# Order of the lo parts and of the products with the values in an attention loop

## Chip, cores and metric

One core of a Trainium2 chip runs the whole kernel. The metric is the device time of one execution in microseconds (us). Five engines have queues of their own, which are worked off in order and wait for one another only through semaphores: TensorE (PE, matmuls and transposes by matmul; PEld are its weight loads), VectorE (DVE), ScalarE (ACT), GpSimd (POOL) and SyncE (SP, which here issues most transfers).

## What is computed

One layer of a decoder trunk in float32: x (1, 1024, 1024) is normalised and projected, goes through three branches (sparse attention, a convolution module, cross-attention into 256 memory tokens), is merged by sigmoid gates, and ends in a SwiGLU feed-forward part. The change lies in the sparse attention, which has 8 heads in 2 groups and three kinds of keys, added up by gates:

```python
s_c = einsum(qq, kc);  p_c = masked_softmax(s_c, cmp_end <= t);   o_c = p_c @ vc    # compressed blocks
idx = top_k(imp_s, 16)                                            # of 16 blocks: all of them
s_s = einsum(qq, ks[idx]);  p_s = masked_softmax(s_s, tok <= t);  o_s = p_s @ vs[idx]   # selected
s_w = einsum(qq, kw);  p_w = masked_softmax(s_w, 0 <= t - pos < 512);  o_w = p_w @ vw   # window
out = gate[0] * o_c + gate[1] * o_s + gate[2] * o_w
```

There are 16 blocks of 64 tokens and 16 are selected, so the selected branch is causal attention over all tokens.

## The kernel before

Every float32 operand of a matmul is taken in two parts: hi, a cast to a shorter format by ScalarE (line 131), and lo, the rest, `src - hi`, by VectorE or GpSimd (line 132). The helper `split` emits the two one behind the other, and all products are sums over hi and lo parts. `mm` (line 146) is the helper that records every matmul, so all of them show as L146; tiles tell them apart.

The attention runs over 16 units (i, g): i counts eight tiles of 128 queries, g the two groups of four heads. A unit takes four steps of the loop: window scores of heads 0 and 1, of heads 2 and 3, then selected scores of heads 0 and 1 (`hp` = 0) and 2 and 3 (`hp` = 1). `scores` makes the score products, the maxima (VectorE, L771; L760 for the 64 compressed keys, which come with the selected ones) and the exponentials (ScalarE, L776 and L762, recorded in `exps`). GpSimd multiplies by the reciprocal sum and the gate (L695).

What follows the scores is put on a list, `due`, under a later step. Four steps after the selected scores of a half come the products with the values, `values`. For a half of the selected branch it goes through the key tiles two by two (a "pair"; i + 1 tiles, so up to four pairs). For each pair:

- up to four transposes (PE, L890) turn the probabilities into a bank of PSUM of pool 1 (`at=1`, two banks, shared with the turned queries and the compressed probabilities);
- the cast (ACT, L131) and the lo part (DVE, L132) go to a tile of the pool `t4` (four buffers, also used for the hi parts of the window);
- per key tile, one product with the hi and one with the lo part are added to the output bank `OB[(i, g)]` (pool 2, two banks).

For the compressed branch all four heads are turned into one bank (L876, 64 partitions), split into the lower and upper 64 partitions of one tile, and one product with `vcmp` adds both parts. It is emitted ahead of the selected products of the first half and has the `start` flag that opens the output bank. Window probabilities take another way: VectorE turns them in squares (L808), SP stores them (L816) and loads them again (L828), GpSimd makes their lo parts, and `window_products` closes the bank. `heads_out` then adds the two halves of the bank (L861, L862) and stores the sum (L864).

Between all this lie fill products: the merge gates' projection, emitted with the lowest priority in banks `pf` (L146 pf, then L948). Each is tied to an entry of `anchors`, a list of products of the attention, so that the fills are spread over it. After the attention come the branches' output projections (L1014 to L1027).

The order of each engine's queue is not the order of emission. The context is opened with `schedule_with_timeline_sim=True`: a planner takes ready instructions by priority (order of emission, unless set otherwise) on a timeline of times that it estimates, gives out buffers as it goes, and so fixes the order of every queue. `follow(m, i, why)` adds to that planning an edge with no semaphore: m is planned behind i.

Of the kernel before, what the change touches and what calls it, by code (L numbers as in the profile page):

```python
# [8 lines left out]
F32 = mybir.dt.float32  # L9
F32R = mybir.dt.float32r  # L10
BF16 = mybir.dt.bfloat16
AF = mybir.ActivationFunctionType
OP = mybir.AluOpType
# [4 lines left out]
P = 128  # L18
# [15 lines left out]
WB, SPREAD = 6, 97  # L34
# [5 lines left out]
def hybrid_layer_kernel(  # L40
# [4 lines left out]
    nc = tc.nc  # L45
# [21 lines left out]
    def nm(s):  # L67
        count[0] += 1
        return f"{s}_{count[0]}"

    def slab(shape, dt=F32R):
        return slabs.tile([P] + shape, dt, tag="slab", name=nm("slab"))
# [13 lines left out]
    def t4(shape, dt=F32):  # L86
        return t4p.tile([P] + shape, dt, tag="t4", name=nm("t4"))

    def t2(shape, dt=F32, p=P):
        return t2p.tile([p] + shape, dt, tag="t2", name=nm("t2"))  # L90
# [8 lines left out]
    def bank(shape, dt=F32, p=P, at=None):  # L99
        if at is None:  # L100
            turn[1] += 1
            at = order[turn[1] % len(order)]
        return psp[at].tile([p] + shape, dt, tag=f"ps{at}", name=nm("ps"))
# [9 lines left out]
    def const(shape, dt, name, p=P):  # L113
        return cp.tile([p] + shape, dt, tag=name, name=name)
# [15 lines left out]
    def split(hi, lo, src, eng=None):  # L130
        m = nc.scalar.copy(hi, src)  # L131
        return m, (eng or nc.vector).tensor_tensor(lo, src, hi.bitcast(F32), op=OP.subtract)  # L132
# [12 lines left out]
    def mm(o, a, b, start, stop):  # L145
        m = nc.tensor.matmul(o, a, b, start=start, stop=stop)  # L146
        n = 1
        for d in o.shape[1:]:
            n *= d
        products.append((m.ins, n if a.dtype == F32R else 4 * n))  # L150
        return m
# [14 lines left out]
    ident = identr.bitcast(F32)  # L166
# [26 lines left out]
    vcmp = const([2, P], F32R, "vcmp")  # L193
# [9 lines left out]
    def follow(m, i, why):  # L203
        tc.add_manual_dep(m.ins, i.name, ORDER, reason=why)
# [164 lines left out]
    b = bank([2 * KT])  # L369
# [10 lines left out]
    for u in range(2):  # L380
        w_ = slab([2, 2, 512])
        m, _ = split(w_[:, 0], w_[:, 1], raw_w[u])
# [20 lines left out]
    b = bank([4, TAPS + 3])  # L403
# [5 lines left out]
    b = bank([2, 16])  # L409
# [45 lines left out]
    b = bank([NT, 24])  # L455
# [83 lines left out]
    for hp in range(2):  # L539
# [7 lines left out]
        b = bank([2, 256])  # L547
# [100 lines left out]
    VSW = [slab([NT, 2, P]) for _ in range(2)]  # L648
# [27 lines left out]
    with low(TAP):  # L676
        along = products[first_tap:]
        total, run, j = sum(n for _, n in along), 0, 0
# [18 lines left out]
    QS, OB, QN, PC, WT, WP, WF, anchors, behind, tails, exps = {}, {}, {}, {}, {}, {}, {}, [], [], [], []  # L697
# [24 lines left out]
    def turn_q(i, g):  # L722
        if g == 0 and i + 1 < NT:
            load_q(i + 1)
        qd = t2([4, 2, 64])
        nc.gpsimd.tensor_tensor(qd, QN[i][:, 4 * g:4 * g + 4, None, :].to_broadcast([P, 4, 2, 64]),
                                rqn[:, i, 4 * g:4 * g + 4, None, None].to_broadcast([P, 4, 2, 64]), op=OP.mult)
        b = bank([4, P], at=1)
        for h in range(4):
            nc.tensor.transpose(b[:, h, :], qd[:, h].rearrange("p a d -> p (a d)"), ident)  # L730
        QT = stage.tile([P, 2, 4, P], F32R, tag="st", name=nm("qt"))
        split(QT[:, 0], QT[:, 1], b)
        QS[(i, g)] = QT
# [86 lines left out]
    def window_load(i, g):  # L820
        full = min(i + 1, 4)
        WT[(i, g)] = slab([4, 4, 4, 32])
        for j0 in range(0, full, 2):
            square_load(WT[(i, g)][:, j0:min(j0 + 2, full)], i, g, j0)
# [33 lines left out]
    def heads_out(i, g):  # L858
        o = OB[(i, g)]
        bot = t2([4, P], p=64)  # L860
        nc.scalar.copy(bot, o[64:128])  # L861
        nc.vector.tensor_tensor(bot, o[0:64], bot, op=OP.add)  # L862
        put = lambda: follow(
            nc.sync.dma_start(od[2 * g:2 * g + 2, :, i * P:(i + 1) * P].rearrange("c (h d) t -> d (c h) t", d=64), bot),  # L864
            exps[-1], "stored behind the last exponential")
        due.setdefault(4 * (2 * i + g) + 10, []).insert(0, put)

    def values(u, tiles):
        i, g, br, hp = u
        if br == 0:  # L870
            OB[(i, g)] = bank([4, P], at=2)
        o = OB[(i, g)]
        if br == 0:
            b = bank([4, P], at=1)
            for h in range(4):
                nc.tensor.transpose(b[:64, h, :], tiles[h], ident)  # L876
            pt = t2([4, P], F32R)
            split(pt[:64], pt[64:], b[:64])
            m = mm(o.rearrange("p h q -> p (h q)"), vcmp[:, g, :], pt.rearrange("p h q -> p (h q)"), True, False)
            anchors.append((3, m.ins))  # L880
            return
        nb = i + 1
        oh = o[:, 2 * hp:2 * hp + 2, :].rearrange("p h q -> p (h q)")
        for j0 in range(0, nb, 2):
            js = range(j0, min(j0 + 2, nb))
            b = bank([2, 2, P], at=1)
            pt = t4([2, 2, 2 * P], F32R)
            for j in js:
                for h in range(2):
                    nc.tensor.transpose(b[:, j - j0, h, :], tiles[h][:, j * P:(j + 1) * P], ident)  # L890
            n = len(js)
            bv = b.rearrange("p j h q -> p j (h q)")
            split(pt[:, 0, :n], pt[:, 1, :n], bv[:, :n])
            for j in js:
                for hl in range(2):
                    m = mm(oh, VSW[0][:, j, g, :], pt[:, hl, j - j0, :], False, False)
        anchors.append((WB + nb, m.ins))

    load_q(0)
    turn_q(0, 0)  # L900
    due = {}
    for n in range(2 * NT):
        i, g = n // 2, n % 2
        for at, br, hp in ((0, 2, 0), (1, 2, 1), (2, 1, 0), (3, 1, 1)):
            step = 4 * n + at
            for f_ in due.pop(step, []):
                f_()
            if (br, hp) == (1, 0) and n + 1 < 2 * NT:
                turn_q((n + 1) // 2, (n + 1) % 2)
            tiles = scores(i, g, br, hp)  # L910
            if br == 2 and hp == 0:
                for late, what, j0 in ((7, window_parts, 0), (8, window_parts, 2), (8, window_products, 0),
                                       (9, window_parts, 4), (9, window_products, 2), (9, window_products, 4)):
                    due.setdefault(step + late, []).append(lambda f=what, i=i, g=g, j0=j0: f(i, g, j0))
                due[step + 9].append(lambda i=i, g=g: heads_out(i, g))
            if br == 2:
                continue
            if hp == 0:
                due.setdefault(step + 4, []).append(lambda i=i, g=g: window_load(i, g))
                due[step + 4].append(lambda u=(i, g, 0, 0): values(u, PC[u[:2]]))  # L920
            due.setdefault(step + 4, []).append(lambda u=(i, g, br, hp), tiles=tiles: values(u, tiles))
    tails.pop()(exps[-1])
    while due:
        for f_ in due.pop(min(due)):
# [10 lines left out]
    with low(FILL):  # L935
        for n_ in range(3 * KT):
# [3 lines left out]
            for h_ in range(2):  # L940
                ps = fbank([512])
                for k in range(KT):
                    first = mm3(ps, w[:, 0, k, :], w[:, 1, k, :], xn(0, k, h_), xn(1, k, h_), k == 0, k == KT - 1)
                    j = ((n_ - N_EARLY) * 2 + h_) * KT + k
# [55 lines left out]
    for n_, (br, wt) in enumerate(branches):  # L1000
        ins = nxt
        for dp in range(4):
# [5 lines left out]
            for d_ in (2 * dp, 2 * dp + 1):  # L1008
# [6 lines left out]
                for half in range(2):  # L1015
# [13 lines left out]
                    if n_ == 2:  # L1029
                        if d_ % 2 == 0:  # L1030
                            MG[half][dp] = slab([2, 2, 512])
                        m = MG[half][dp]
# [51 lines left out]
    js = [[None] * 2 for _ in range(4)]  # L1084
# [72 lines left out]
    for c in range(2):  # L1157
# [4 lines left out]
        for t in range(NT):  # L1162
# [17 lines left out]
            h = H[tp][:, tt, cs]  # L1180
# [231 lines left out]
```

## Time and profile before

| what | value |
|---|---|
| median of three runs | 1691.99 us (1691.52 to 1693.93) |
| profiled execution | 1692.24 us, its span 1690.5 us |
| mean granted TensorE clock | 0.997 |
| busy: PE, PEld | 1658.4 us, 1382.6 us |
| busy: DVE, ACT, POOL | 1061.2, 727.2, 583.8 us |
| attention loop | about 430 to 800 us of the span |

Rows of the profile name engine, line, operation and tiles (output <- inputs), with buffer numbers left out: `t` are tiles of t4 or t2, `ps` banks of PSUM, `slab` and `wsl` larger tiles. In a row of waits stand the sum in us, the number of times and the longest; in an order of time the start, the duration, and in brackets the idle time of the engine ahead of it and what ended it. In a group's row the busy time, the mean in ns of one, then the idle time ahead of them.

### The profile page before, as it was taken

The numbers are of one execution on the slowest core, as the hardware profiler recorded it, in microseconds if no ns is written. First come the engines' busy times: TensorE is split into PE (matmuls) and PEld (weight loads), VectorE is DVE, ScalarE is ACT, GpSimd is POOL, SyncE is SP. The second block draws the span as 40 slices with busy tenths as digits, with TensorE's granted clock in tenths as the row PEclk, the third lists the DMA queues.
The fourth block names the chain that finished last, engine by engine and source line by source line (L and its number), as shares of the span: only waits on it lengthen the run. The fifth ranks groups of instructions, "written<-read, shape, count | busy, mean of one in ns | idle before, by whom it ended". The sixth has DMA issues, their size and how long they took to land.

```text
span 1690.5 us, 22456 instructions
## 1 busy us (share of the span) xinstructions
PE 1658.4 (98%) x8064; PEld 1382.6 (82%) x8064; DVE 1061.2 (63%) x1811; ACT 727.2 (43%) x1340; POOL 583.8 (35%) x514
## 2 busy tenths in 40 slices
PE   7999999999999999999989999999999999999999
PEld 6887898888888888887868888788888888888887
DVE  6278897678456777766567535864544545466655
ACT  6311443343366767676446324532222222233332
POOL 0000000110167777674016401566556776400000
PEclk9999999999999999999999999999999999999999
DMA  8012443312155555456555223233233445793763
GB/s 283 34 40 88 156 138 112 112 57 87 43 144 151 153 172 158 138 152 200 188 193 172 90 87 107 87 121 98 94 106 123 163 144 187 276 399 119 234 223 125
DMA packets 217173, 243.23 MB, mean 144 GB/s; under 512 B 13332, under 2 KB 146756, under 8 KB 216038
## 3 DMA queue, kind: packets, MB, share of 16 engines
q1 hardware_dynamic: 210150, 229.22, 42.5%
q10 hardware_dynamic: 6912, 12.59, 2.0%
q8 instruction: 63, 1.03, 0.3%
q14 instruction: 48, 0.39, 0.1%
HBM read 171.50 MB, written 70.25 MB: 143 GB/s over the span
## 4 chain that ended last, share of the span: by engine, by line
PE 56%; DVE 2%; DMA 1%; ACT 1%; issue 1%; SPq 0%; POOL 0%; ACTq 0%
PE ps L146 35%; PE ps L1346 11%; PE pf L146 7%; PE pf L1346 1%; DVE slab L132 1%; PE ps L890 1%; SPq L816 0%; ACT slab L131 0%; DMA st<-md 0%; DMA t<-zd 0%; DMA st<-in_w_mem_out_dram 0%; DVE t L128 0%; PE ps L233 0%; ACT fz L948 0%; DVE slab L1181 0%
## 5 line engine op out<-in xcount | busy, mean ns | idle before, releaser
L146 PE MATMUL ps<-slab,wsl 128*128 128x512 f32 (+1 forms) x1580 | 351.6, 381 | 1.8 <-ACT wsl L131 0.7
L146 PEld LDWEIGHTS ps<-slab,wsl 128*128 128x128 f32 x1580 | 286.7, 188 | 60.7 <-ACT wsl L131 1.1
L146 PE MATMUL pf<-slab,fsl 128*128 128x512 f32 x1260 | 326.2, 399 | 4.5 <-DVE slab L971 2.6
L146 PEld LDWEIGHTS pf<-slab,fsl 128*128 128x128 f32 x1260 | 230.5, 189 | 51.4 <-ACT fz L948 4.4
L146 PE MATMUL ps<-slab,fsl 128*128 128x512 f32 x708 | 165.9, 390 | 0.0
L1242 DVE TENSOR_TENSOR t<-ps,t 128x512 f32<-128x512 f32 x130 | 89.0, 689 | 118.0 <-PE ps L146 116.9
L146 PEld LDWEIGHTS ps<-slab,fsl 128*128 128x128 f32 x708 | 132.6, 188 | 27.6
L422 DVE SCALAR_TENSOR_TENSOR slab<-slab,cw 128x1021 f32<-128x1021 f32 (+15 forms) x120 | 151.6, 1265 | 1.9
L146 PE MATMUL ps<-wsl,slab 128*128 128x512 f32 (+1 forms) x690 | 148.5, 362 | 0.0
L146 PE MATMUL ps<-slab,slab 128*128 128x512 f32 x532 | 139.2, 397 | 3.3 <-POOL slab L132 1.1
L146 PEld LDWEIGHTS ps<-wsl,slab 128*128 128x128 f32 x690 | 115.8, 189 | 18.6
L594 POOL TENSOR_SCALAR t<-t,sm 128x256 f32<-128x256 f32 x32 | 17.9, 578 | 298.9 <-DVE sm L590 281.8
L146 PEld LDWEIGHTS ps<-slab,slab 128*128 128x128 f32 x532 | 100.2, 190 | 25.5 <-DVE slab L225 1.8
L1346 PE MATMUL ps<-wsl 128*128 128x512 f32 x492 | 118.0, 389 | 0.0
L1346 PEld LDWEIGHTS ps<-wsl 128*128 128x128 f32 x492 | 92.4, 188 | 19.1
L146 PE MATMUL ps<-t,slab 128*128 128x256 f32 (+1 forms) x500 | 104.4, 313 | 0.8 <-DVE t L132 0.7
L132 DVE TENSOR_TENSOR wsl<-st,wsl 128x1024 fp32r<-128x1024 f32 x58 | 74.4, 1285 | 36.4 <-ACT wsl L131 36.2
L132 DVE TENSOR_TENSOR t<-ps,t 128x512 fp32r<-128x512 f32 (+2 forms) x120 | 77.3, 649 | 31.8 <-ACT t L131 31.0
L131 ACT CAST wsl<-st 128x1024 fp32r<-128x1024 f32 x58 | 60.9, 1050 | 84.0 <-PE ps L146 36.4
L146 PE MATMUL ps<-slab,qt 128*128 128x384 f32 (+6 forms) x400 | 93.6, 339 | 1.4 <-DVE sm L771 0.9
L146 PEld LDWEIGHTS ps<-t,slab 128*128 128x128 f32 x500 | 78.0, 189 | 9.5 <-DVE t L132 2.3
L131 ACT CAST t<-ps 128x512 fp32r<-128x512 f32 (+2 forms) x120 | 65.1, 554 | 44.1 <-PE ps L890 25.0
(255 smaller groups left out, 2763.7 us busy)
## 6 DMA issues: line engine op xcount, KB each, us to landing
t<-in_w_down_dram SPq DMA_DIRECT2D x70, 256.0 KB, 3.9
fst<-in_w_in_dram SPq DMA_DIRECT2D x24, 512.0 KB, 3.9
zd<-fz ACTq DMA_DIRECT2D x48, 256.0 KB, 2.5
slab<-wd SPq DMA_DIRECT2D x24, 512.0 KB, 4.8
t<-zd SPq DMA_DIRECT2D x24, 512.0 KB, 4.1
st<-in_w_gate_dram SPq DMA_DIRECT2D x22, 512.0 KB, 3.7
st<-in_w_up_dram SPq DMA_DIRECT2D x22, 512.0 KB, 4.2
ad<-t SPq DMA_DIRECT2D x44, 256.0 KB, 2.7
```

Of the source, the lines that this page charges most:

```text
L131: m = nc.scalar.copy(hi, src)
L132: return m, (eng or nc.vector).tensor_tensor(lo, src, hi.bitcast(F32), op=OP.subtract)
L146: m = nc.tensor.matmul(o, a, b, start=start, stop=stop)
L422: return nc.vector.scalar_tensor_tensor(acc[:, s:], u[:, :S - s], cw[:, ct, 30 - s:31 - s], acc[:, s:], op0=OP.mult, op1=OP.add)
L594: nc.gpsimd.tensor_scalar(pm[:, tt, h, :], pm[:, tt, h, :], rec[:, j:j + 1], 1.0, op0=OP.mult, op1=OP.mult)
L890: nc.tensor.transpose(b[:, j - j0, h, :], tiles[h][:, j * P:(j + 1) * P], ident)
L1242: nc.vector.tensor_tensor(o, a_, b_, op=OP.add)
L1346: nc.tensor.matmul(B[t], a_, b_, start=start and k == 0 and j == 0, stop=k == FH - 1 and j == 2, skip_group_check=True)
```

## The change

The cast of each selected pair stays where it was. Its lo part is no longer emitted with it, but put on a list `pend`, and emitted after the cast of the next pair, with a planning edge behind that cast; the pair's products with the values come behind the lo part. The first product of the first half of the selected branch has the `start` flag. The compressed probabilities are turned and cast behind the second half (`short_values`, one step later than before); their lo part and product are emitted at the beginning of the next step, planned behind the last exponential. Anchors are recorded with the products, now in their new order.

```diff
+    def flush(after):
+        todo = list(pend)
+        pend.clear()
+        for f_ in todo:
+            f_(after)
+
+    def low_part(o, b, hi, after):
+        follow(nc.vector.tensor_tensor(o, b, hi.bitcast(F32), op=OP.subtract), after, "low part behind the next cast")
+
+    def short_values(i, g):
+        tiles = PC[(i, g)]
+        b = bank([4, P], at=1)
+        for h in range(4):
+            nc.tensor.transpose(b[:64, h, :], tiles[h], ident)
+        pt = t2([4, P], F32R)
+        flush(nc.scalar.copy(pt[:64], b[:64]).ins)
+
+        def rest(after):
+            low_part(pt[64:], b[:64], pt[:64], after)
+            m = mm(OB[(i, g)].rearrange("p h q -> p (h q)"), vcmp[:, g, :], pt.rearrange("p h q -> p (h q)"), False,
+                   False)
+            anchors.append((3, m.ins))
+
+        pend.append(rest)
+
     def values(u, tiles):
         i, g, br, hp = u
-        if br == 0:
+        if hp == 0:
             OB[(i, g)] = bank([4, P], at=2)
         o = OB[(i, g)]
-        if br == 0:
-            b = bank([4, P], at=1)
-            for h in range(4):
-                nc.tensor.transpose(b[:64, h, :], tiles[h], ident)
-            pt = t2([4, P], F32R)
-            split(pt[:64], pt[64:], b[:64])
-            m = mm(o.rearrange("p h q -> p (h q)"), vcmp[:, g, :], pt.rearrange("p h q -> p (h q)"), True, False)
-            anchors.append((3, m.ins))
-            return
...
             bv = b.rearrange("p j h q -> p j (h q)")
-            split(pt[:, 0, :n], pt[:, 1, :n], bv[:, :n])
-            for j in js:
-                for hl in range(2):
-                    m = mm(oh, VSW[0][:, j, g, :], pt[:, hl, j - j0, :], False, False)
-        anchors.append((WB + nb, m.ins))
+            flush(nc.scalar.copy(pt[:, 0, :n], bv[:, :n]).ins)
+
+            def rest(after, js=js, j0=j0, n=n, pt=pt, bv=bv):
+                low_part(pt[:, 1, :n], bv[:, :n], pt[:, 0, :n], after)
+                for j in js:
+                    for hl in range(2):
+                        m = mm(oh, VSW[0][:, j, g, :], pt[:, hl, j - j0, :], hp == 0 and j == 0 and hl == 0, False)
+                if js[-1] == nb - 1:
+                    anchors.append((WB + nb, m.ins))
+
+            pend.append(rest)
...
-                due[step + 4].append(lambda u=(i, g, 0, 0): values(u, PC[u[:2]]))
             due.setdefault(step + 4, []).append(lambda u=(i, g, br, hp), tiles=tiles: values(u, tiles))
+            if hp == 1:
+                due[step + 4].append(lambda i=i, g=g: short_values(i, g))
+                due.setdefault(step + 5, []).insert(0, lambda: flush(exps[-1]))
```

More of the change, by code (lines that the diff above doesn't have):

```diff
@@ L892, in values @@
             bv = b.rearrange("p j h q -> p j (h q)")
-            split(pt[:, 0, :n], pt[:, 1, :n], bv[:, :n])
-            for j in js:
-                for hl in range(2):
-                    m = mm(oh, VSW[0][:, j, g, :], pt[:, hl, j - j0, :], False, False)
-        anchors.append((WB + nb, m.ins))
+            flush(nc.scalar.copy(pt[:, 0, :n], bv[:, :n]).ins)
[7 more added lines that the diff above has]
+            pend.append(rest)
     load_q(0)
     turn_q(0, 0)
-    due = {}
+    due, pend = {}, []
     for n in range(2 * NT):
```

## The prediction

> **What bounds the kernel now.** I read the page first (busy shares, then the chain), then the stretch that holds the attention loop in the table of windows, then the waits of that stretch one engine at a time, and last the order of time around two of the waits.
>
> ```profile
> PE 1658.4 (98%) x8064; PEld 1382.6 (82%) x8064; DVE 1061.2 (63%) x1811; ACT 727.2 (43%) x1340; POOL 583.8 (35%) x514
> PE 56%; DVE 2%; DMA 1%; ACT 1%; issue 1%; SPq 0%; POOL 0%; ACTq 0%
> ```
>
> ```profile
> core 0: us, PE busy (x) PEld busy (x) DVE busy (x) ACT busy (x) POOL busy (x), PEclk, DMA share, GB/s
> 430.00:800.00 370.00, 361.48 (x2009) 306.63 (x2007) 244.21 (x818) 247.40 (x605) 238.44 (x254) 1.00 0.50 147
> ```
>
> The reader is to see that TensorE (PE) sets the time and that the attention, about 430 to 800 us, is no exception: there the matmuls fill 361.48 of 370 us, VectorE 244 and ScalarE 247, at a granted clock of 1.00. So a matmul moved from one place to another is worth nothing; only stretches in which PE stands still are. Those are these (a wait of the weight load, PEld, and one of the matmul are two views of the same stop, so the two lists are not added):
>
> ```profile
> PEld ps L146 <- DVE t L132: 7.2, 14, 1.1
> PEld pf L146 <- ACT fz L948: 2.8, 8, 0.5
> PEld ps L146 <- DVE sm L771: 1.9, 5, 0.8
> PE ps L146 <- DVE t L132: 2.8, 8, 0.7
> ```
>
> The largest cause is "t L132" on VectorE, the lo part of a split. It holds PE 14 times. Which products wait is told by the groups of instructions from 430 to 830 us:
>
> ```profile
> L146 PEld LDWEIGHTS ps<-t,vcmp 128*128 128x128 f32 x16 | 3.0, 188 | 5.1 <-DVE t L132 4.9
> L146 PEld LDWEIGHTS ps<-t,slab 128*128 128x128 f32 x374 | 58.9, 189 | 7.4 <-DVE t L132 2.3
> ```
>
> So 4.9 us belong to the 16 products with the compressed values (those that open the output bank) and 2.3 us to the products that read selected (and window) probabilities. Two of the first kind and one of the second, in order of time:
>
> ```profile
> 661.04 0.19 PEld L146 LDWEIGHTS ps<-t,vcmp 128*128 128x128 f32 x1 [0.64 <-DVE t L132]
> ...
> 764.66 0.58 ACT L131 CAST t<-ps 64x512 fp32r<-64x512 f32 x1
> 764.67 0.68 DVE L862 TENSOR_TENSOR t<-ps,t 64x512 f32<-64x512 f32 x1 [0.72 <-ACT t L861]
> 765.28 0.73 DVE L771 CUSTOM_DVE_ANT_0 slab<-ps,strip,sm 128x512 f32<-128x512 f32 x1
> 765.70 0.58 ACT L131 CAST t<-ps 128x512 fp32r<-128x512 f32 x1
> 766.05 0.69 DVE L132 TENSOR_TENSOR t<-ps,t 64x512 fp32r<-64x512 f32 x1
> 766.07 0.30 PEld L146 LDWEIGHTS ps<-slab,qt 128*128 128x128 f32 x2 [0.43 <-DVE sm L771]
> 766.79 0.19 PEld L146 LDWEIGHTS ps<-t,vcmp 128*128 128x128 f32 x1 [0.42 <-DVE t L132]
> 779.67 0.57 ACT L131 CAST t<-ps 128x512 fp32r<-128x512 f32 x1
> 780.27 0.69 DVE L132 TENSOR_TENSOR t<-ps,t 128x512 fp32r<-128x512 f32 x1 [0.81 <-ACT t L131]
> 781.02 0.53 PEld L146 LDWEIGHTS ps<-t,slab 128*128 128x128 f32 x4 [0.42 <-DVE t L132]
> ```
>
> In the middle one the cast was ready at 765.24, but VectorE took the lo part at 766.05, behind two other instructions of its queue, and PE, which had the compressed product next, stood for 0.42 us. In the last VectorE itself stood 0.81 us for the cast, and PE 0.42 us for the lo part.
>
> **The change, part by part.** It adds and removes no engine work and no transfer: the same 64 + 16 casts and lo parts of selected scores, 16 + 16 of the compressed ones, the same transposes and products. Only positions change. The kernel's planner puts each queue in order from the order of emission and from times it estimates, so a new order of emission changes the order on PE, ACT, DVE and, behind them, on POOL and SP too.
>
> ```profile
> L132 DVE TENSOR_TENSOR t<-ps,t 128x512 fp32r<-128x512 f32 x64 | 43.6, 685 | 26.6 <-ACT t L131 26.4
> L132 DVE TENSOR_TENSOR t<-ps,t 64x512 fp32r<-64x512 f32 x16 | 10.9, 684 | 0.7 <-ACT t L131 0.2
> L132 DVE TENSOR_TENSOR t<-ps,t 128x256 fp32r<-128x256 f32 x16 | 6.7, 416 | 2.7 <-ACT t L131 2.6
> L131 ACT CAST t<-ps 128x512 fp32r<-128x512 f32 x64 | 36.8, 580 | 19.0 <-PE ps L890 18.3
> ```
>
> (1) Lo parts of selected pairs behind the next pair's cast. At present VectorE waits 26.4 + 2.6 us in these rows for the cast just ahead of the lo part. With a cast in between (580 ns) that wait should mostly go; VectorE is busy 244 of 370 us, so its own time is worth nothing, but what is queued behind it (maxima, L771, on which PE waited 1.9 us) comes sooner. I count none of this.
>
> (2) Selected products behind that lo part. PE meets, between a pair's transposes and its products, the next pair's four transposes and whatever the planner puts there. Removes the 2.3 us, and what could be late next is the transposes two pairs on, which need the bank (two of them, `at=1`) that the lo part releases.
>
> (3) Compressed values last, their lo part behind the last exponential of the step, their product a step later. A step is some 6.6 us here (from the compressed product at 661.04 to the fourth after it, at 766.79, are sixteen steps), against 0.68 us for the lo part: removes the 4.9 us. Late next: nothing before the window products, which end the bank.
>
> (4) The first selected product opens the bank: the `start` flag moves from one matmul to another, nothing on any engine. It also frees the selected products from the wait for all four compressed tiles.
>
> (5) Fill products are tied to anchors, which now sit on later products of the same pair; the count and weights stay, so I take 0, covered by the products that now stand ahead of them. If that cover failed, the row to look at is "pf L146", whose wait for ACT is 2.8 us now.
>
> The sum. How much streaming is lost in a stop lies between the matmul list and the weight-load list: 2.8 and 7.2 us. The row below (from the chain) gives 0.23 us for 512 columns.
>
> ```profile
> 760.57 2.75 PE pf L146 x12
> ```
>
> Ahead of the stop at 766.79 the weights of two score products came at 766.07; the two, of 448 columns, stream 0.40 us, to about 766.47, 0.1 us into the idle of 0.42 that began at 766.37. So about three quarters of the idle is real: 0.75 x 7.2 = 5.4 us, which I take.
>
> New waits: nothing in the trace shows a product behind a later cast. Bound from below by 0, from above by a full extra cast on every pair whose transposes need a bank still held: pairs per half are 1, 1, 2, 2, 3, 3, 4, 4 for the eight query tiles, so 24 pairs stand third or later in their half (1 + 1 + 2 + 2, times two halves, times two groups), 24 x 0.58 = 13.9 us. The nearest row is the present wait of transposes, which shows PE standing on L890 only 0.5 us in all, because fills lie between; I take 0.8 us. Net: -5.4 + 0.8 = -4.6 us. Against the profiled execution (1692.24 us; its span 1690.5 and 1.74 around it) that is 1687.6; that execution stands 0.25 us above the median of 1691.99, so 1687.4 against the median.
>
> ```profile
> L890 PE MATMUL ps<-identr,slab 128*128 128x128 f32 x288 | 45.0, 272 | 0.5 <-DVE qt L132 0.5
> ```
>
> [...] The change holds each selected bank for one more cast. [...] No run of the present order can show it, and the second rival prices it from rows.
>
> **Rivals.** First, no change that can be measured (0.2% is 3.4 us): the idle goes from the attention and comes back where something else ends last. For it speaks what follows the attention:
>
> ```profile
> 863.64 1.13 PE L146 MATMUL pf<-slab,ones 128*128 128x512 f32 x2 [1.74 <-ACT fz L948]
> 867.34 4.61 PE L146 MATMUL pf<-slab,fsl 128*128 128x512 f32 x12 [2.57 <-DVE slab L971]
> 872.53 0.74 PE L146 MATMUL ps<-slab,wsl 128*128 128x512 f32 x2 [0.59 <-DVE slab L1025]
> ```
>
> Here PE stands 1.74 + 2.57 + 0.59 = 4.9 us: the last fill's result goes to memory and back before the branch can use it. If the fills end as late as now, or the last pair's longer way to its output pushes this stretch by as much as was won, the sum is about 0: 1692. Against it: PE, not these transfers, carries 56% of the chain.
>
> Second, slower: selected pairs are held one cast longer, in the two `at=1` banks and in the four `t4` tiles, of which the window parts take up to two. Place: the transposes (L890) of pair three and on in a half, and their casts (L131). Price: 0.58 us for each of the 24, if no fill lies ready. It decides when more than (4.6 + 3.4) / 0.58 = 14 of them are uncovered; with 18 it is -4.6 + 10.4 = +5.8, 1697.8, with all 24, 1701. For it: ACT already waits for these transposes 18.3 us (row above). Against: fills are spread over the whole attention and the pairs in which two or fewer are wanted don't meet it.
>
> Third, a larger gain. The compressed transposes hold one of the two `at=1` banks for long, because half of them come early:
>
> ```profile
> 646.66 0.38 PE L876 MATMUL ps<-identr,t 128*64 128x128 f32 x2
> 653.60 0.38 PE L876 MATMUL ps<-identr,t 128*64 128x128 f32 x2
> ```
>
> Over 14 us pass from the first transposes to the product (661.04, above), and the selected pairs go through the other bank. Emitted last, they would leave both banks to the selected pairs. The rest of the list of the weight load's waits:
>
> ```profile
> PEld ps L876 <- POOL t L695: 1.4, 2, 1.2
> PEld ps L146 <- POOL slab L132: 1.4, 1, 1.4
> PEld ps L146 <- PE ps L146: 1.0, 2, 0.6
> PEld ps L890 <- DVE qt L132: 0.8, 1, 0.8
> PEld ps L730 <- issue: 0.8, 1, 0.8
> PEld ps L146 <- ACT qt L131: 0.6, 1, 0.6
> ```
>
> With the 7.2 + 2.8 + 1.9 above it comes to 17.9 us; if half of the 10.7 us that are not lo parts went as well, 1687.4 - 5.4 = 1682.0.
>
> **How the numbers follow.** Forecast 0.45 (its own range 1684.8, all 7.2 us gone, to 1689.2, only 2.8), of which I put 0.36 below the bound of 3.4 us and 0.09 within it; first rival 0.22; second 0.24; third 0.09. Faster 0.36 + 0.09 = 0.45, same 0.09 + 0.22 = 0.31, slower 0.24. The predicted time is the forecast's, 1687.4. The range reaches to the third rival below (1682.0 less some 1.5) and above to where the second has 18 to 20 of its 24: 1680.5 to 1698.5; cases of both signs hold it.
>
> **What would show it.** Right: "t L132" gone or under 2 us among PE's waits in the attention, no idle ahead of the products with the compressed values, VectorE's wait for "t L131" far below 29 us, and the end of the attention's products some 5 us earlier. Wrong: a wait of L890 on "DVE t L132", or of L146 "ps" on something new, of several us; ACT waiting more than 18 us on L890; or an attention that is shorter and a stretch after 860 us that has grown. The forecast also fails if the new order on POOL or SP moves the window stores and loads (L816, L828) so that window products wait for them.

## Result and profile after

The changed kernel takes 1708.98 us (1707.16 to 1711.87, four runs) against 1692.43 us: a ratio of 1.0095, interval 1.0082 to 1.0107, or 16.6 us slower. The forecast was 1687.4 us, faster, with a range to 1698.5. A trace is of one of the timed executions, not of the median: 1709.83 us here, and in the experiments below 1706.24 us with the queries in another pool and 1710.16 us with the last unit at once, each the slowest of its kind.

In the changed kernel the lines of the attention have moved: L890 is now L906 (transposes of the selected pairs), L876 is L881, the cast and the lo part of the selected pairs are L909 and L875 (those of the compressed probabilities L883 and L875), L948 is L972. Page, then the attention and what follows it:

```profile
PE 1667.8 (98%) x8064; PEld 1389.0 (81%) x8064; DVE 1062.0 (62%) x1811; ACT 731.9 (43%) x1342; POOL 580.2 (34%) x514
PE 73%; DVE 5%; DMA 2%; issue 2%; ACT 1%; POOL 1%; SPq 0%; DVEq 0%; POOLq 0%; ACTq 0%
```

```profile
430.00:800.00 370.00, 355.44 (x1943) 1.00 0.47 136
800.00:900.00 100.00, 92.25 (x405) 0.93 0.61 209
```

The columns of the second fence are the stretch, its length, PE's busy time with its count, granted clock, share of the transfers and GB/s. The work is the same (8064 matmuls), but between 430 and 800 us 66 fewer of them (1943 for 2009) got done, with 355.44 us busy for 361.48. Behind 800 us the kernel before had this:

```profile
800.00:900.00 100.00, 94.39 (x407) 0.98 0.58 193
```

In the attention PE's weight loads wait for other things than before:

```profile
PEld ps L146 <- DVE sm L771: 8.9, 13, 1.6
PEld ps L146 <- DVE t L875: 6.2, 16, 1.8
PEld ps L146 <- ACT qt L131: 5.1, 8, 0.9
PEld ps L906 <- DVE qt L132: 3.2, 10, 0.5
PEld ps L146 <- issue: 2.5, 4, 1.6
```

The wait for lo parts has only fallen from 7.2 to 6.2 us, and two waits have grown: for the maxima (L771) from 1.9 to 8.9 us, and for the turned queries (`qt`, cast and lo part) from 0.6 + 0.8 to 5.1 + 3.2 us. The same by group, from 430 to 830 us:

```profile
L146 PEld LDWEIGHTS ps<-t,slab 128*128 128x128 f32 x361 | 61.3, 189 | 15.0 <-DVE t L875 8.3 <-ACT t L909 0.5
L146 PEld LDWEIGHTS ps<-t,vcmp 128*128 128x128 f32 x15 | 2.8, 188 | 0.9 <-DVE t L875 0.5
```

The compressed products hardly wait any more (4.9 to 0.5 us), as forecast; the selected products, which were to lose 2.3 us of waiting, now have 8.3, of which one stop at 810 us, behind the stretch above, is 2.6.

How the queries come late is seen in order of time, at the end of a first half (query tile 6, whose last pair has one key tile, so two transposes and a cast of 256):

```profile
722.24 0.38 PE L906 MATMUL ps<-identr,slab 128*128 128x128 f32 x2
...
722.91 0.36 ACT L909 CAST t<-ps 128x256 fp32r<-128x256 f32 x1
723.14 0.69 DVE L875 TENSOR_TENSOR t<-ps,t 128x512 fp32r<-128x512 f32 x1
...
724.34 0.60 PE L730 MATMUL ps<-identr,t 128*128 128x128 f32 x4
724.98 0.59 ACT L131 CAST qt<-ps 128x512 fp32r<-128x512 f32 x1 [0.42 <-PE ps L730]
725.62 0.47 PEld L146 LDWEIGHTS ps<-slab,qt 128*128 128x128 f32 x3 [0.76 <-ACT qt L131]
...
726.37 0.41 DVE L875 TENSOR_TENSOR t<-ps,t 128x256 fp32r<-128x256 f32 x1
```

The half's last pair is transposed at 722.24, and its lo part comes at 726.37: its bank is held for 4.5 us, though the cast was done at 723.27. The queries' transposes (724.34) come behind the lo part of the pair before (723.14 to 723.83), which frees the other bank, and the next score products need those queries at once: PE's weight loads stand 0.76 us for them, its matmuls 0.56.

### The profile page after: what moved, and what is told of

Same layout as the page of the kernel before. It is cut to its first block, busy times and chain, and to the rows that moved or that the text cites. A ratio compares the mean times of both kernels' runs of the same rounds, so it can differ in the third digit from the quotient of the medians.

```text
span 1708.1 us, 22461 instructions
## 1 busy us (share of the span) xinstructions
PE 1667.8 (98%) x8064; PEld 1389.0 (81%) x8064; DVE 1062.0 (62%) x1811; ACT 731.9 (43%) x1342; POOL 580.2 (34%) x514
## 4 chain that ended last, share of the span: by engine, by line
PE 73%; DVE 5%; DMA 2%; issue 2%; ACT 1%; POOL 1%; SPq 0%; DVEq 0%; POOLq 0%; ACTq 0%
PE ps L146 42%; PE pf L146 16%; PE ps L1370 11%; PE ps L906 1%; PE pf L1370 1%; DVE slab L771 1%; DVE slab L132 1%; DMA wd<-wsl 1%; ACT slab L131 1%; POOL slab L1052 1%; DVE wsl L808 1%; PE ps L604 0%; DMA t<-zd 0%; DVE t L875 0%; DMA st<-md 0%
## 5 line engine op out<-in xcount | busy, mean ns | idle before, releaser
L146 PE MATMUL ps<-slab,wsl 128*128 128x512 f32 (+1 forms) x1580 | 355.8, 384 | 1.2 <-ACT wsl L131 0.7
L146 PE MATMUL pf<-slab,fsl 128*128 128x512 f32 x1260 | 315.1, 394 | 1.5 <-ACT fz L972 1.5
L146 PE MATMUL ps<-t,slab 128*128 128x256 f32 (+1 forms) x500 | 118.3, 322 | 9.2 <-DVE t L875 8.9
L146 PEld LDWEIGHTS ps<-t,slab 128*128 128x128 f32 x500 | 82.9, 190 | 22.3 <-DVE t L875 13.2
L132 DVE TENSOR_TENSOR wsl<-st,wsl 128x1024 fp32r<-128x1024 f32 x58 | 75.7, 1306 | 37.9 <-ACT wsl L131 37.5
L132 POOL TENSOR_TENSOR slab<-slab,t 128x1024 fp32r<-128x1024 f32 (+1 forms) x28 | 62.6, 2235 | 65.7 <-ACT t L131 49.4
L146 PEld LDWEIGHTS ps<-slab,qt 128*128 128x128 f32 x400 | 63.7, 189 | 22.4 <-DVE sm L771 8.7
```

## Experiments

The theory I began with, 'bank held': a bank of the transposes that waits for a later cast before its lo part is one bank less for the next pairs and for the queries. Rivals: the later products themselves, the later place of the compressed probabilities, or lo parts at a bad place in VectorE's queue. Times are medians, ratios against runs of the kernel before on the same chip.

**Nothing deferred, compressed probabilities last.**

```diff
-            flush(nc.scalar.copy(pt[:, 0, :n], bv[:, :n]).ins)
+            cast = nc.scalar.copy(pt[:, 0, :n], bv[:, :n]).ins
...
-            pend.append(rest)
+            rest(cast)
```

(the same two lines in `short_values`)

> Nothing is deferred here: each lo part and its products follow their own cast, as before the change; what stays of the change is that the compressed probabilities come last, behind the second half, and that the first selected product opens the output bank. Theory 'bank held' (the two banks of the transposes are each held until the next pair's cast, so that pairs no longer overlap): this does not hold a bank longer, so within 5 us of before, 1687 to 1695 us, and PE waits less than 3 us for DVE sm L771. Theory 'compressed last' (the later place of the compressed probabilities makes the unit longer): 1703 us or more.

1689.01 us, ratio 0.9976 (0.9967 to 0.9985): faster. In the attention the weight loads' waits for L771 are 1.4 us, and the compressed products wait for no lo part. So the later place of the compressed probabilities and the new opening product are not the loss; alone they bring 3.4 us.

**The deferral alone.** `short_values` has `split` and its product at once, opens the bank, and stands ahead of the first half.

> The deferral alone: the compressed probabilities come first and open the output bank, as before the change; lo parts and products of the selected pairs come behind the next pair's cast, as in the change. Theory 'bank held': it has all of the cause, 1703 to 1713 us, with PE waiting over 5 us for DVE sm L771. Theory 'compressed last': 1688 to 1696 us.

1715.49 us, ratio 1.0134 (1.0118 to 1.0150). Slower than the change itself, so all of the loss is here, and a little above the range given:

```profile
PEld ps L146 <- ACT qt L131: 13.3, 12, 1.6
PEld ps L146 <- DVE t L875: 10.9, 22, 1.5
PEld ps L146 <- DVE sm L771: 7.1, 12, 1.2
```

The wait for turned queries is the largest of all.

**Lo parts with their casts, products deferred** (the same in `short_values`).

```diff
-            flush(nc.scalar.copy(pt[:, 0, :n], bv[:, :n]).ins)
+            cast = nc.scalar.copy(pt[:, 0, :n], bv[:, :n]).ins
+            low_part(pt[:, 1, :n], bv[:, :n], pt[:, 0, :n], cast)
+            flush(cast)
             def rest(after, js=js, j0=j0, n=n, pt=pt, bv=bv):
-                low_part(pt[:, 1, :n], bv[:, :n], pt[:, 0, :n], after)
```

> As the change, but the lo part of each selected pair (and of the compressed probabilities) stands again right behind its own cast and so gives its bank back at once; only the products come behind the next pair's cast. Theory 'bank held': the loss is gone, 1685 to 1694 us. Theory 'late products' (products that come a pair or a step later lengthen every unit, delay the fills tied to them and the last pair): the loss stays, 1703 us or more.

1685.27 us, ratio 0.9957 (0.9942 to 0.9972). 'Late products' falls: with the products as late as in the change the kernel is 23.7 us faster than the changed one and 7.1 us faster than before. Only the lo parts differ. If nothing but the planning edge of the lo parts (the `follow`) is left out of the change, the planner gives every queue the same order as here; so it is the edge that does the harm, not the place of the lo part in the text.

**Nothing held over the end of a half.** The last pair of a half and the compressed probabilities are not deferred; pairs within a half are.

> As the change, but nothing is held over the end of a half: the last pair of a half and the compressed probabilities have lo part and products right behind their own cast; between pairs of one half the deferral stays. Theory 'bank held': the 24 pairs third or later in a half still meet a held bank, and the bank that was held over a step is free, so between the two: 1696 to 1704 us. If it is the bank held over a step alone (queries are turned in the same two banks): 1688 to 1695 us, and the PE waits for ACT qt L131 and DVE qt L132 fall below 2 us from 8 us.

1689.99 us, ratio 0.9984 (0.9974 to 0.9994), and the waits for queries are 1.0 and 0.7 us. That is in the range for a bank held over a step alone, and below the one for any held bank. The deferral between pairs of one half, on which the second rival of the prediction had put its price, costs hardly anything (1689.01 us with nothing deferred). What costs is a bank held over a step.

**Three banks for the transposes**, with a control.

```diff
-    cnt = [3, 2, 2]
+    cnt = [3, 3, 1]
...
-    pools = ([0, 0, 0, 2], [1, 1, 2, None])
+    pools = ([0, 0, 0, 2], [1, 1, 1, None])
```

> The change, with three banks of PSUM instead of two for the transposes (pairs, turned queries, compressed probabilities); one bank is taken from the output banks, which stays one, and the last stage's list of banks is adapted. To be read against the kernel before with the same banks (next run). Theory 'bank held': a third bank makes up for the one that is held, so within 5 us of that control. Rival 'lo parts in the wrong place of VectorE's queue', whatever the banks: 10 us or more above the control.

> Control: the kernel before with three banks for the transposes and one output bank. Both theories: 1684 to 1700 us; it only serves as the base of the run above.

The change with three banks takes 1685.07 us, the kernel before with three banks 1682.33 us (ratios to before 0.9957, 0.9942 to 0.9972, and 0.9939, 0.9924 to 0.9953). Of 16.6 us of loss 2.7 are left. The lo parts have the same planning edge and still start 2.2 us behind the end of their casts in the mean (2.5 us with two banks), so their late place in VectorE's queue is not the cause by itself; the shortage of banks is.

**Queries in another pool.**

```diff
-        b = bank([4, P], at=1)
+        b = bank([4, P], at=2)
         for h in range(4):
             nc.tensor.transpose(b[:, h, :], qd[:, h].rearrange("p a d -> p (a d)"), ident)
```

> The change, with the turned queries in the banks of the output pool instead of those of the transposes. Theory 'queries starve' (the bank held over a step leaves the queries' transposes no bank until just before their use): PE's waits for ACT qt L131 and DVE qt L132 (5.1 and 3.2 us with the change) fall below 1.5 us in all, waits for DVE sm L771 below 4 us, and the time falls by 6 to 10 us, to 1699 to 1703 us; what is left is behind 800 us. Rival 'pairs no longer overlap': 1705 us or more.

1700.66 us (1696.46 to 1706.24), ratio 1.0047 (1.0032 to 1.0062): 8.3 us of the 16.6 come back, as expected, and no wait for the turned queries is left among PE's. But the wait for maxima stays at 6.1 us, not below 4, so it is only in part a consequence of late queries, and between 800 and 900 us the same loss is seen as with the change (92.34 us busy for 92.25).

**Last unit at once.** Nothing is deferred for query tile 7, second group.

> The change, but in the last of the 16 units (query tile 7, second group) nothing is deferred. Theory 'tail': the two waits of PE for the lo parts at 810 and 837 us (7.4 us, behind the layer norm's work in VectorE's queue) and the lower granted clock behind them (0.66 and 0.74 for 10 us each) go: 1696 to 1702 us. Theory that the tail only shows what the attention lost earlier: 1705 us or more.

1704.93 us (ratio 1.0071, 1.0054 to 1.0087): 4 us less than the change, where at least 7 were expected; the time lies between the two ranges. The two waits named are gone, but for 0.7 us, and another place is there behind 800 us, one that the kernel before has too:

```profile
PEld pf L146 <- DVE slab L999: 3.4, 1, 3.4
PEld pf L146 <- ACT fz L976: 2.2, 1, 2.2
```

Before the change PE's weight loads wait there 3.4 us for L971 and, the longest, 2.2 us for L948, the same lines of the code. That a part of the tail's gain is given back there is likely, but not shown: in the profiled execution the mean granted clock from 430 to 800 us was also 0.99, where it is 1.00 with the change.

**Only the first half at once.** Its last pair is not held to the second half; all else is as in the change.

```diff
+        if hp == 0:
+            flush(cast)
```

> The change, but the last pair of the first half has its lo part and products right behind its own cast; the last pair of the second half still waits for the compressed cast, and the compressed probabilities still for the next step. Theory 'the bank held from the first half to the second starves the queries' (the queries are turned in that same step): PE's waits for ACT qt L131 and DVE qt L132 fall from 8.3 us to under 2 us and the time to 1688 to 1695 us. Rival 'it is the compressed probabilities that are held over': 1700 us or more.

Here `cast` is that of the half's last pair. 1687.98 us, ratio 0.9970 (0.9959 to 0.9980): 21.0 us faster than the change, with the lo part and the products of one pair in each unit let go earlier (that the place of the products costs nothing is shown by the third experiment). PE's waits for queries fall to 0.3 + 0.4 us, for maxima to 1.8:

```profile
PEld ps L146 <- DVE t L875: 5.0, 15, 1.0
PEld pf L146 <- ACT fz L975: 2.0, 5, 0.6
PEld ps L146 <- DVE sm L771: 1.8, 6, 0.5
PEld ps L146 <- ACT t L909: 1.6, 4, 0.5
PEld ps L146 <- ACT t L762: 1.2, 1, 1.2
PEld ps L906 <- DVE qt L132: 0.4, 2, 0.3
PEld ps L146 <- PE ps L146: 0.3, 1, 0.3
PEld ps L146 <- ACT qt L131: 0.3, 1, 0.3
```

The rival, that the compressed probabilities held to the next step are the cause, falls. The planned order of PE's queue says why. This is how much time of matmuls stands in it between the transposes of a unit's queries and their first use, in the mean of the last 14 units. It is an estimate: the matmuls between the two are counted at 0.456 ns a column and at least 109 ns each, about the distance from start to start of fills and of transposes in the traces (12 fills of 512 columns take 2.75 us before the change, 0.45 ns a column; four transposes 0.60 us at 724.34 after it, one of them 0.27, so 0.11 us from one to the next).

```
before                          4.1 us
change                          1.6 us
deferral alone                  0.7 us
only the first half at once     4.4 us
change, three banks             6.7 us
```

A unit's queries are turned in the step in which the first half's values of the unit two before stand (at 724.34 us those of query tile 7, beside the values of tile 6, first group), and in the same two banks. With one of the two tied to the cast of the second half, one step on, the planner puts the queries' transposes late, close to their use.

**Three banks and products only.** The third experiment and the three banks together.

> Both gains together: lo parts with their own casts, products behind the next pair's cast, compressed probabilities last, and three banks for the transposes. If the gains add (7.1 us and 9.9 us against before): 1675 to 1679 us. If both take away the same waits: 1681 to 1684 us, as the control with three banks.

1679.19 us, ratio 0.9921 (0.9908 to 0.9935). The gains add in part: 13.2 us below before, against 7.1 and 9.9 for each. The wait for lo parts in the attention is down to this:

```profile
PEld ps L146 <- DVE t L875: 1.2, 3, 0.5
```

## Why the prediction was wrong

What bounds the kernel was read rightly: PE, by its stops. The step that failed is (2), and with it the term of 0.8 us for new waits. It named the right resource, the two `at=1` banks that the lo part gives back, but looked for the late work among "the transposes two pairs on", and priced the second rival on the 24 pairs that stand third or later in a half. These are still deferred in "Only the first half at once", which is faster than before. The turned queries use the same two banks and were left out, though the order of steps puts them beside the first half's values; and the last pair of a half waits not for one more cast of 0.58 us but for a cast a step later (its bank was held for 4.5 us at 722.24). In place of 0.8 us of new waits the runs show 21.0 us that go when that one pair of each first half is let go at once, and 8.3 us that go when only the queries get other banks. Two signs of being wrong that the prediction named came: PE waits several us for something new (`qt`), and ScalarE waits 35.9 us, for 18.3, on the transposes.

- (1) VectorE's wait for the casts of the selected pairs did fall, from 26.4 + 2.6 us to 8.3 (from 430 to 830 us); a new one stands ahead of the compressed lo parts (L883). What that fall alone is worth, which the prediction counted as nothing, no run separates:

```profile
DVE t L875 <- ACT t L883: 10.6, 8, 2.7
DVE t L875 <- ACT t L909: 8.3, 6, 3.2
```

- (2) 2.3 us were to go; 8.3 us are there. The 0.5 us of PE's waits at the selected transposes, from which the 0.8 was taken, is 0.6 us now, and on the weight load's side 3.2 us for 0.8. That row could not show the price, because in the order before no bank was held over a step; but it named `DVE qt L132`, the queries' lo part, as what the transposes waited for, and so the other user of the banks.
- (3) and (4) held: the compressed products' wait fell from 4.9 to 0.5 us (15 of the 16 lie before 830 us now), and compressed last with the new opening product, with nothing deferred, brings 3.4 us (ratio 0.9976). The sum for the whole kernel, 4.6 us, is close to what the first half at once gives (4.4 us), but by chance: 5.0 of the 7.2 us of waits for lo parts are left there, and the gain comes from elsewhere.
- The first rival's place, the stop behind 860 us, is not in the change's trace. The runs with the last unit at once and with nothing deferred have it (3.4 + 2.2 us in both); the second of them is faster than before all the same, so it doesn't take back the whole of a gain.
- The third rival, that the early compressed transposes keep a bank from the selected pairs, fits the run with nothing deferred, and three banks alone bring 9.9 us; which part of that is the pairs' and which the queries' was not tried.

For the tail the sum had nothing; only the first rival spoke of the last pair's longer way to its output. With the change two more stops come there, and 4 us of the loss go with the last unit at once. Around the later one, in order of time:

```profile
833.41 3.07 DVE L986 TENSOR_TENSOR slab<-slab,slab 128x1024 f32<-128x1024 f32 x1 [4.99 <-DMA slab<-ud]
836.40 0.68 DVE L875 TENSOR_TENSOR t<-ps,t 128x512 fp32r<-128x512 f32 x1
837.13 1.01 PE L146 MATMUL ps<-t,slab 128*128 128x256 f32 x3 [4.68 <-DVE t L875]
837.94 4.59 PE L146 MATMUL ps<-slab,wsl 128*128 128x512 f32 x12
842.37 2.88 PE L146 MATMUL pf<-slab,fsl 128*128 128x512 f32 x12
```

A lo part moved behind the layer norm's addition in VectorE's queue, which itself stood 4.99 us for a transfer, and PE stood for it. The run with the last unit at once takes this stop away.

What stays open: how much of the wait for maxima (8.9 us; 6.1 with the queries elsewhere, 1.8 with the first half at once) comes from the pairs and how much from scores that start late; so the way from the held bank to the loss is shown for the queries, some half of it, and not for the rest; and the last 2.7 us between change and control with three banks.

## What to carry to other kernels

Before moving a read of a PSUM bank behind later work, list every user of that pool of banks, not only the next of the same kind, and ask over which step of the loop the bank is now held. In this kernel moving the consumer (the products, which read from four buffers) did no harm (ratio 0.9957); moving the release of one of two banks did (1.0095, and 1.0134 by itself). If PE's waits for something prepared well ahead, like turned queries, grow, look at the lead that the plan gives it and at who has its buffer.

## Hardware, not expected

With the change, two stops of PE come with a lower granted clock and with slower products behind them. By stretches of 10 us (start and end, length, PE's busy time and count, clock, share of the transfers, GB/s):

```profile
800.00:810.00 10.00, 7.75 (x43) 1.00 0.69 250
810.00:820.00 10.00, 9.17 (x31) 0.66 0.97 358
820.00:830.00 10.00, 10.00 (x58) 1.00 0.18 61
830.00:840.00 10.00, 5.32 (x24) 0.74 0.36 100
840.00:850.00 10.00, 10.00 (x42) 0.92 0.43 144
```

Behind the stop of 2.36 us that ended at 810.12 the clock is 0.66, in the stretch with that of 4.68 us 0.74 (0.50 from 838 to 840); the 12 products at 837.94 take 4.59 us, 12 of the same size at 842.37 only 2.88, so that the first 12 took some 1.7 us more. The many stops below 2 us in the change's attention left the clock at 1.00, the longest, of 1.56 us, among them (it ended at 671.14; 1.00 from 672 to 680). But the length of a single stop did not decide it in these runs. In the kernel before, a stop of 1.41 us, with two of 0.4 us behind it, was followed by a lower clock; with the deferral alone, one of 2.93 us was not. Each is shown with the clock of the stretch around it:

```profile
1078.15 0.50 PE L146 MATMUL pf<-slab,u 128*128 128x512 f32 x1 [1.41 <-ACT t L1072]
1079.00:1084.00 5.00, 4.50 (x9) 0.54 0.28 81
824.96 6.09 PE L146 MATMUL ps<-slab,wsl 128*128 128x512 f32 x24 [2.93 <-ACT wsl L131]
820.00:830.00 10.00, 7.00 (x38) 1.00 0.87 287
830.00:840.00 10.00, 10.00 (x57) 1.00 0.30 105
```

What decides is not shown by these runs.
